# Two-layer transformer trunk on one Trainium2 core: both o-projection stages in written order with three early token tiles, the next x turned on chip, and squares, totals and o weights at other places

## The chip, the cores and the metric

One core of one Trainium2 chip runs the whole program in one launch. Its engines are TensorE (PE, matrix products), VectorE (DVE), ScalarE (ACT) and GpSimd (POOL); SyncE (SP) issues most of the DMAs. The metric is the device time of one execution in microseconds. Each engine works through its own instruction stream in order, and engines wait for one another through semaphores.

## The reference

S = 1024 tokens, D = 1024, 8 heads, a feed-forward width of 4096, all in float32. Two layers: layer A mixes tokens with multi-head latent attention, layer B with differential attention (two causal softmax maps per head). Cut to what matters:

```python
ALPHA = (2 * DEPTH) ** 0.25          # sqrt(2)
for i in range(2):
    m = (_mla if i == 0 else _diff_attn)(x, ...)      # ends with  o @ w_o
    x = layernorm(ALPHA * x + m, ln_mix_g[i], ln_mix_b[i])
    x = layernorm(ALPHA * x + square(relu(x @ w_up[i])) @ w_down[i], ln_ffn_g[i], ln_ffn_b[i])
```

A LayerNorm takes mean and variance over D of each token, with an epsilon of 1e-5 under the root.

## The kernel before

**Stages.** In the profiled execution layer A's attention runs to about 382 us, its o-projection and the start of its FFN to 516, the FFN's up loop to 806 and the down stage to 1128; then come layer B's eight heads (to 1523), the drain of the last head (to 1578), B's o-projection (to 1707), the up loop (to 1998), the down stage and the last LayerNorms (to 2310).

**Tiles.** Tokens are cut into 8 tiles of 128. Every float32 product is three fp16 products of high and low halves (`mm3`, `p3`), so each weight and each activation is scaled and split on the way: ACT writes the high half (`scaled_split`, L264) and DVE the low half (L265). `tp_...` names are transpositions on PE (eight or four 128x128 blocks); each result is evicted by ACT (L264) and DVE (L265) in the same manner.

**o-projection.** `out_proj` returns `scan` (squares of the o weights, for their scale), `scale`, `weights` (load and split of one of 8 row blocks) and `tile_steps`. For one token tile those are: `start` (load the attention's output and the residual row, and multiply the row by ALPHA on POOL, L320), eight `products` (48 matmuls of 128x512), and `end` (residual sum on DVE, L230; squares for the variance on ACT, L239; the root's few steps). `ln_apply` (L247, L250) finishes the LayerNorm on DVE. The first two tiles are done inside the attention's end, the other six after it. Each finished row X is stored to DRAM, and turned for the FFN: tiles 0 to 3 as they are (B11, B21), tiles 4 to 7 as well (B22) and as four sums with tiles 0 to 3 (T1 to T4, made by `x_sums` on POOL).

**FFN.** Up and down products use seven products in place of eight 2x2-blocked ones: for each of 16 groups g the up products are `u_p1` to `u_p7` into PSUM banks a, b, c and d; `pu` (L1039) is the ACT eviction of `u_p1`, and `u_p6` needs its bank. `u_p7(0)` is the first product of the loop over g. In that loop `up_load`, `up_sq`, `up_add`, `up_cast`, `up_scale` and `up_split` prepare the up weights three groups ahead (names `wuA_r`, `junkA`, `wuA`), `u_out` forms on POOL and stores the hidden rows (`hs`), and `wd_scan` loads the group's down weights and squares them on ACT (`wdsA`, `wdsB`). The totals of these squares give the down weights' scale (`down_scale`: reduce and cast on DVE, one matmul with ones, `tot_cd..`, then a root). The down stage takes 7 products of 8 steps (m, st_); `h16` and `w16` are the operands' splits, `add_y` (L1229) adds a product to X, and `fin_...` end the layer. In layer A `to_xt` turns each finished x for the next layer; tiles 6 and 7 are loaded again from `x1_d` at the start of the differential attention and turned there.

**Who sets the order.** A scheduler with a timeline model of its own orders each engine's instructions, except inside `with in_order():`, where PE, DVE, ACT and POOL keep the order in which the code is written. Before, the up loop, the down stage and the start of the differential attention were under it, and the o-projection stages were not. DMA queues are always the scheduler's. Of buffers, the token rows, the squares' rows (`wds`, `junk`) and the hidden rows share one ring of 8 (`row`), and raw loads of weights one of 3.

## Time and profile before

| what | value |
|---|---|
| median of 3 runs | 2306.92 us (2303.02 to 2308.64) |
| profiled execution, time | 2311.53 us |
| its span in the profile | 2309.8 us |
| mean clock granted to PE | 0.969 of full speed |
| busy: PE, DVE, ACT, POOL | 92%, 73%, 56%, 23% |

The span is the time from the first to the last instruction of the profiled execution, so 1.7 us of its time lie around it. A busy share is a mean over all stages. The granted clock of 1 stands for 2.4 GHz, and half of it for 1.2 GHz.

### The profile page before, as it was taken

To read this page: it belongs to the slowest core of one execution; us is meant where nothing else is said; L and a number is where in the kernel's file an instruction comes from. 1 tells how busy PE (TensorE), PEld (TensorE's weight loads), DVE (VectorE), ACT (ScalarE), POOL (GpSimd) and SP (SyncE) were. 2 spreads that over 40 slices of the span, in tenths; PEclk is the share of its full clock that TensorE was granted. 3 is DMA by queue.
4 is the path that set the end of the run, shared out by engine and by line. 5 is a ranking of instruction groups with operands and counts; after the bars stand their busy time and mean duration, and the time that the engine had idled before them with its cause. 6 is when DMAs were issued, how large, how long until landed. Compare 5 with 4: busy or idle time off the path is not lost. (4 is left out here: it accounts for less than half of the span.)

```text
span 2309.8 us, 31741 instructions
## 1 busy us (share of the span) xinstructions
PE 2136.2 (92%) x11255; PEld 1191.6 (52%) x11255; DVE 1684.8 (73%) x2951; ACT 1300.7 (56%) x2400; POOL 529.1 (23%) x381
## 2 busy tenths in 40 slices
PE   7999898989999899999699999969989999999997
PEld 7878775444444344444356655644444444444443
DVE  5677675767777579877578888784857776588787
ACT  5465664446666355446388777673455665354443
POOL 1101001816666310000000001000826666300000
PEclk9999999989999999999899999988989999999999
DMA  4154767526666776652565565455436666856641
GB/s 146 33 104 91 147 123 188 194 101 205 207 213 207 264 281 218 201 192 82 160 155 126 126 122 106 84 118 150 162 142 205 209 210 223 326 198 210 218 155 55
DMA packets 454831, 384.29 MB, mean 166 GB/s; under 512 B 251376, under 2 KB 346624, under 8 KB 454672
## 3 DMA queue, kind: packets, MB, share of 16 engines
q1 hardware_dynamic: 452736, 376.51, 55.2%
q0 software_dynamic: 1936, 5.75, 0.9%
q8 instruction: 88, 1.44, 0.3%
q14 instruction: 71, 0.58, 0.1%
HBM read 247.97 MB, written 83.89 MB: 144 GB/s over the span
## 5 line engine op out<-in xcount | busy, mean ns | idle before, releaser
L185 PE MATMUL yA<-w16A,h16A 128*128 128x512 f16 x1344 | 294.9, 382 | 4.4 <-DVE X2A L1229 3.1
L185 PE MATMUL yB<-w16B,h16B 128*128 128x512 f16 x1344 | 292.8, 380 | 4.6 <-DVE X2B L1229 3.1
L185 PE MATMUL qkv<-wqkv,xt_nA 128*128 128x384 f16 x1536 | 268.5, 328 | 1.0 <-DVE wqkv L265 0.7
L185 PEld LDWEIGHTS <-wuB 128*128 128x128 f16 x1344 | 132.1, 99 | 172.0 <-issue 18.1
L185 PEld LDWEIGHTS <-wuA 128*128 128x128 f16 x1344 | 132.2, 99 | 170.9 <-issue 16.0
L185 PEld LDWEIGHTS <-h16A 128*128 128x128 f16 x1344 | 132.2, 98 | 167.3 <-issue 12.5
L185 PEld LDWEIGHTS <-h16B 128*128 128x128 f16 x1344 | 131.8, 98 | 168.1 <-issue 11.4
L185 PEld LDWEIGHTS <-xt_nA 128*128 128x128 f16 x1536 | 150.0, 99 | 95.8 <-issue 4.4
L1585 DVE TENSOR_REDUCE nmx_d<-ds 128x2 f32<-128x256 f32 (+5 forms) x96 | 90.1, 951 | 24.0 <-PE ds L413 23.6
L265 DVE SCALAR_TENSOR_TENSOR h16B<-hrB,SCB,h16B 128x1024 f16<-128x1024 f32 x56 | 73.3, 1308 | 37.8 <-ACT h16B L264 37.2
L265 DVE SCALAR_TENSOR_TENSOR h16A<-hrA,SCA,h16A 128x1024 f16<-128x1024 f32 x56 | 73.8, 1317 | 35.5 <-ACT h16A L264 35.4
L264 ACT ACTIVATE h16A<-hrA,SCA 128x1024 f16<-128x1024 f32 x56 | 63.9, 1141 | 61.0 <-issue 47.9
L264 ACT ACTIVATE h16B<-hrB,SCB 128x1024 f16<-128x1024 f32 x56 | 63.9, 1140 | 59.9 <-issue 47.9
L413 PE MATMUL s<-kn,qn 128*128 128x512 f32 (+2 forms) x288 | 83.5, 385 | 8.3 <-DVE ph L427 7.8
L185 PE MATMUL oA<-woA,otA 128*128 128x512 f16 x384 | 86.7, 387 | 4.1 <-DVE ph L427 4.1
L185 PE MATMUL oB<-woB,otB 128*128 128x512 f16 x384 | 85.4, 379 | 0.0
L265 DVE SCALAR_TENSOR_TENSOR wuB<-wuB_s,cuB,wuB 128x1024 f16<-128x1024 f32 (+1 forms) x32 | 56.7, 1771 | 34.9 <-ACT wuB L264 34.9
L185 PE MATMUL av_d<-pt16d,dv 128*128 128x256 f16 (+1 forms) x480 | 59.3, 277 | 24.4 <-DMA pt16d<-phd 24.4
L265 DVE SCALAR_TENSOR_TENSOR wuA<-wuA_s,cuA,wuA 128x1024 f16<-128x1024 f32 (+1 forms) x32 | 54.9, 1716 | 34.9 <-ACT wuA L264 34.9
L264 ACT ACTIVATE w16B<-wdB,RBB 128x1024 f16<-128x1024 f32 x40 | 45.7, 1142 | 53.5 <-DVE wdB L1186 53.5
L264 ACT ACTIVATE w16A<-wdA,RBA 128x1024 f16<-128x1024 f32 x40 | 45.7, 1141 | 53.4 <-DVE wdA L1186 53.4
L1489 POOL MEMSET ones_f<- 128x128 f32 x1 | 0.2, 205 | 305.3 <-PE yA L185 305.3
(876 smaller groups left out, 5099.1 us busy)
## 6 DMA issues: line engine op xcount, KB each, us to landing
hrA<-hs_d SPq DMA_DIRECT2D x56, 512.0 KB, 3.8
hrB<-hs_d SPq DMA_DIRECT2D x56, 512.0 KB, 3.8
wuA_r<-in_ffn_w_up_dram SPq DMA_DIRECT2D x32, 512.0 KB, 4.5
wdsA<-in_ffn_w_down_dram SPq DMA_DIRECT2D x32, 512.0 KB, 6.5
wdA<-in_ffn_w_down_dram SPq DMA_DIRECT2D x32, 512.0 KB, 4.7
wuB_r<-in_ffn_w_up_dram SPq DMA_DIRECT2D x32, 512.0 KB, 4.3
wdsB<-in_ffn_w_down_dram SPq DMA_DIRECT2D x32, 512.0 KB, 5.9
wdB<-in_ffn_w_down_dram SPq DMA_DIRECT2D x32, 512.0 KB, 4.6
```

The source lines that it names most:

```text
L185: nc.tensor.matmul(dst, l, r, start=first and m == 0, stop=last and m == n - 1, skip_group_check=resumed)
L264: nc.scalar.mul(hi, src, scale)
L265: nc.vector.scalar_tensor_tensor(out=lo, in0=src, scalar=scale, in1=hi, op0=ALU.mult, op1=ALU.subtract)
L413: nc.tensor.matmul(dst, q_, k_(c0 // 512, n), start=m == 0, stop=m == len(pairs) - 1)
L1489: nc.gpsimd.memset(ones_f, 1.0)
L1585: nc.vector.tensor_reduce(out=nmx[:, ms], in_=st["wide"][:, :, :nk] if i < 4 else st[m], axis=AX.X, op=ALU.max, negate=True)
```

## The change

The residual is no longer multiplied by ALPHA: the o-projection's and the down stage's scales are divided by ALPHA instead, and the LayerNorm's epsilon by ALPHA squared, which gives the same LayerNorm. After the attention both o-projection stages stand under `in_order()`, and a third token tile moves inside the attention's end. The load of the squares' rows (`wd_fetch`) is cut from the squares (`wd_scan`); the reduce and cast of the down scale (`down_sum`) stand earlier than its matmul. Tiles 6 and 7 of the next x are turned right after their LayerNorm. Layer B's o weights are scanned and loaded one head earlier.

The diff, cut to its core:

```diff
+            nc.vector.tensor_scalar(out=icw, in0=icw, scalar1=1.0 / ALPHA, scalar2=None, op0=ALU.mult)
...
-                nc.gpsimd.tensor_scalar(out=t["x"], in0=t["x"], scalar1=ALPHA, scalar2=None, op0=ALU.mult)
...
-            def end():
-                nmean = residual(t["y"], icw, t["x"], f"m{nm}{i}")
-                st[i] = t["x"], nmean, ln_stats(t["x"], nmean, t["y"], f"m{nm}{i}")
-
-            return [(0.1, start)] + [(1.3, lambda k=k: products(k)) for k in range(H)] + [(0.1, end)]
+            def sums():
+                t["m"] = residual(t["y"], icw, t["x"], f"m{nm}{i}")
+
+            def squares():
+                t["q"] = ln_ssq(t["x"], t["m"], t["y"], f"m{nm}{i}")
+
+            def root():
+                st[i] = t["x"], t["m"], rstd_of(t["q"], 1.0 / D, LN_EPS_A, f"ln_m{nm}{i}")
...
+                + [(0.1, sums), (0.1, squares), (0.1, root)]
...
+            return o_steps(u - 3, lambda: x_t(u - 3)) if u - 3 < 3 else []
...
+            def wd_fetch(g):
+                wds[g] = [row(f"wds{nm}{g}{f_}") for f_ in range(2)]
+                for f_ in range(2):
+                    nc.sync.dma_start(out=wds[g][f_], in_=wdn[:, g, f_, :])
+
             def wd_scan(g):
...
-                for f_ in range(2):
-                    wr = row(f"wds{nm}{g}{f_}")
-                    nc.sync.dma_start(out=wr, in_=wdn[:, g, f_, :])
+                for f_, wr in enumerate(wds.pop(g)):
                     nc.scalar.activation(wr, wr, AF.Square, accum_out=wdsq[g // 2][:, 2 * (g % 2) + f_ : 2 * (g % 2) + f_ + 1])
...
-            new_xc()
-            order = [0, 1, 4, 5, 2, 6, 3, 7]
-            for n, i in enumerate(order):
-                X[i] = row(f"X{nm}{i}")
-                if n >= n_early:
-                    for _, step in o_steps(i, lambda i=i: X[i]):
-                        step()
+            order = [0, 1, 2, 4, 5, 6, 3, 7]
...
+            def begin(n):
+
+                if n < NT:
+                    i = order[n]
+                    X[i] = row(f"X{nm}{i}")
+                    if n >= n_early:
+                        todo[n] = [step for _, step in o_steps(i, lambda: X[i])]
+                        todo[n].pop(0)()
...
-                if n == 2:
-                    up_load(0)
-                    up_sq(0)
-                    up_add(0)
-                    up_cast(0)
...
-                    up_add(2)
...
+            def turn(n):
...
-                    to_xc("B11", X[i], i)
-                    to_xc("B21", X[i][:, 512:], i)
-                else:
-                    if n == NT - 1:
-                        for g in range(2):
-                            u_p1(g)
-                            u_p2(g)
-                    t = x_sums(i - 4, nc.gpsimd if n < NT - 1 else nc.vector)
-                    for key, src in (("T2", t[:, 1]), ("T1", t[:, 0]), ("T3", t[:, 2]), ("T4", t[:, 3]), ("B22", X[i][:, 512:])):
-                        to_xc(key, src, i - 4)
-
-
-            wd_scan(0)
-            u_p6(0)
-            u_p5(0)
...
+                    return [lambda: to_xc("B11", X[i], i), lambda: to_xc("B21", X[i][:, 512:], i)]
+                t = xsum[i - 4]
+                rows = (("B22", X[i][:, 512:]), ("T2", t[:, 1]), ("T1", t[:, 0]), ("T3", t[:, 2]), ("T4", t[:, 3]))
+                return [lambda key=key, src=src: to_xc(key, src, i - 4) for key, src in rows]
...
+            prepare = {
+                3: ([lambda: up_prepare(0)], []),
+                4: ([lambda: up_cast(0)], [lambda: up_scale(0), lambda: up_split(0, 0), lambda: up_split(0, 1)]),
+                5: ([lambda: up_split(0, 2), lambda: up_split(0, 3)], [lambda: up_prepare(1)]),
+                6: ([lambda: up_cast(1)], [lambda: up_scale(1)]),
+                7: ([], [lambda: wd_fetch(0), lambda: up_load(2), lambda: (up_sq(2), up_add(2)), lambda: wd_scan(0)]),
+            }
+            with in_order():
+                for n in range(n_early + 2):
+                    begin(n)
+                for n in range(n_early):
+                    normal(n)
+                new_xc()
+                for n in range(n_early, NT + 1):
+                    begin(n + 2)
+                    before, after = prepare.get(n, ([], []))
+                    for step in before:
+                        step()
+                    turns = turn(n - 2)
+                    if n == n_early:
+                        turns = turn(0) + turns
+                    if n < NT:
+                        for _ in range(4):
+                            todo[n].pop(0)()
+                    else:
+                        for step in turns:
+                            step()
+                        turns = []
+                        u_p1(0)
+                        u_p2(0)
+                    if n > n_early:
+                        sums_, squares_, root_ = todo[n - 1]
+                        sums_()
+                        squares_()
+                    if turns:
+                        turns.pop(0)()
+                    else:
+                        up_split(1, 0)
+                    if n > n_early:
+                        root_()
+                        normal(n - 1)
+                        if order[n - 1] >= 4:
+                            i = order[n - 1] - 4
+                            xsum[i] = x_sums(i, nc.gpsimd if n < NT else nc.vector)
+                    if n < NT:
+                        for step in todo[n][:4]:
+                            step()
+                        del todo[n][:4]
+                    for step in turns + after:
+                        step()
+                u_p1(1)
+                u_p2(1)
+                for step in turn(NT - 1):
+                    step()
+                u_p6(0)
+                up_split(1, 1)
+                u_p5(0)
+                up_split(1, 2)
+                up_split(1, 3)
+
...
                     if g + 3 < NG:
                         up_load(g + 3)
                     if g + 1 < NG:
-                        wd_scan(g + 1)
+                        wd_fetch(g + 1)
                     if w:
                         up_cast(g + 2)
+                    if g == NG - 2:
+                        down_sum(NA, "A")
                     if 0 < g < NG - 1:
                         u_p1(g + 1)
...
                         u_p5(g + 1)
+                        wd_scan(g + 1)
                     u_out(g)
...
-                    if (m, st_) == (0, 4):
-                        for i in range(NT):
-                            nc.scalar.mul(X[i], X[i], ALPHA)
...
+                    if (m, st_) == (0, 0):
+                        down_sum(NS, "B")
                     if (m, st_) == (0, 2):
                         down_scale(NS, "B")
...
-                            if layer == 0 and i > 0:
+                        else:
+                            if layer == 0 and i in (1, 2):
                                 to_xt(xt_n, i - 1, "n", ps_wide)
-                        else:
                             fin_rstd(i)
                             fin_apply(i)
-                    if m == 6 and st_ == 1 and layer == 0:
-                        to_xt(xt_n, 3, "n")
+                    if m == 6 and st_ in (1, 2) and layer == 0:
+                        to_xt(xt_n, 1 + st_, "n")
...
+                if layer == 0:
+                    to_xt(xt_n, 6, "n")
                 fin_apply(7)
+                if layer == 0:
+                    to_xt(xt_n, 7, "n")
...
+            if (h, u) in ((H - 2, 0), (H - 2, 2)):
+                steps = merge(steps, [(0.1, lambda k=k: wo_scan(k)) for k in range(2 * u, 2 * u + 4)])
+            if (h, u) == (H - 2, 3):
+                steps.append((0.1, wo_scale))
             if h == H - 1:
-                steps += [(0.1, lambda k=k: wo_scan(k)) for k in range(4 * u, 4 * u + 4)]
+                steps = merge(steps, [(0.1, lambda k=k: wo_load(k)) for k in range(2 * u, 2 * u + 2)])
...
-                return [(0.1, wo_scale)] + [(0.1, lambda k=k: wo_load(k)) for k in range(H)]
+                return [(0.1, lambda k=k: wo_load(k)) for k in range(4, H)]
...
+            return [s for i in range(*((0, 1), (1, 3))[u - 3]) for s in o_steps(i, lambda: x_t(i))]
...
-            xn = [wp.tile([P, D], F32, tag="raw", name=f"x1_{t}", bufs=3) for t in range(2)]
-            for t in range(2):
-                nc.gpsimd.dma_start(out=xn[t], in_=x1_d[(6 + t) * P : (7 + t) * P, :])
...
-                if t in (1, 2):
-                    transpose_in16(xn[t - 1], xt1[1], t + 1, f"nA{5 + t}", sx[:, 2:3])
...
-    mixer_out_and_ffn(1, ws, None, o_steps, o_state, 2, out[0], "B")
+    mixer_out_and_ffn(1, ws, None, o_steps, o_state, 3, out[0], "B")
```

**The up loop.** The squares keep their place on ACT; their loads move against the weights' loads. ACT in the first iteration of the loop of layer A, before (`junk` are squares of the up weights read by `wuA_r`, `pu` the eviction for which `u_p6` waits):

```order
L940 ACTIVATE junkA_5558,wssqA_5557<-wuA_r_5482 128x1024
L940 ACTIVATE junkA_5558,wssqA_5557<-wuA_r_5483 128x1024
L1080 ACTIVATE hA_5376<-hA_5376 128x512
L1081 ACTIVATE hA_5376,hsA_5552<-hA_5376 128x1024
L264 ACTIVATE wuA_3_5582<-wuA_s_5259,cuA_5509 128x512
L1122 ACTIVATE wdsA_5615,wdsqA_5614<-wdsA_5615 128x1024
L1122 ACTIVATE wdsA_5618,wdsqA_5614<-wdsA_5618 128x1024
L1039 ACTIVATE puA_5635<-abA_5349,cuA_5509 128x512
```

ACT at the same place now:

```order
L949 ACTIVATE junkA_5550,wssqA_5549<-wuA_r_5476 128x1024
L949 ACTIVATE junkA_5550,wssqA_5549<-wuA_r_5477 128x1024
L1089 ACTIVATE hA_5348<-hA_5348 128x512
L1090 ACTIVATE hA_5348,hsA_5544<-hA_5348 128x1024
L265 ACTIVATE wuA_3_5574<-wuA_s_5299,cuA_5501 128x512
L1136 ACTIVATE wdsA_5480,wdsqA_5304<-wdsA_5480 128x1024
L1136 ACTIVATE wdsA_5481,wdsqA_5304<-wdsA_5481 128x1024
L1048 ACTIVATE puA_5626<-abA_5321,cuA_5501 128x512
```

SP's queue before, around the load that those squares read (`wdsA_5615` and `wdsA_5618`):

```order
L1121 DMA wdsA_5486<-in_ffn_w_down_dram 128x1024
L1121 DMA wdsA_5489<-in_ffn_w_down_dram 128x1024
L1121 DMA wdsA_5615<-in_ffn_w_down_dram 128x1024
L1121 DMA wdsA_5618<-in_ffn_w_down_dram 128x1024
L931 DMA wuA_r_5610<-in_ffn_w_up_dram 128x8x128
L931 DMA wuA_r_5611<-in_ffn_w_up_dram 128x8x128
```

SP's queue now, around the load that they read now (`wdsA_5480` and `wdsA_5481`):

```order
L940 DMA wuA_r_5476<-in_ffn_w_up_dram 128x8x128
L1307 DMA x_d<-XA_4937 128x1024
L1129 DMA wdsA_5480<-in_ffn_w_down_dram 128x1024
L1129 DMA wdsA_5481<-in_ffn_w_down_dram 128x1024
L1183 DMA wrA_7640<-in_ffn_w_down_dram 128x4x512
L940 DMA wuA_r_5477<-in_ffn_w_up_dram 128x8x128
L1129 DMA wdsA_5608<-in_ffn_w_down_dram 128x1024
```

Before, the squares' load was the last one asked for ahead of them, and stood ahead of `wuA_r_5610`, the weights of group 3. Now it stands one iteration earlier; the load that now has the old place (`wdsA_5608`, `wdsA_5609`) is squared an iteration later.

**The end of o-projection A.** ACT before, from the evictions of the last tile but one to those of the last (`tp_fA3B` and `tp_fA3T` are the transpositions of tiles 3 and 7, `puA` and `hA` evictions of `u_p1` and `u_p2`):

```order
L264 ACTIVATE xB22A<-tp_fA2B_5176,xs_c 128x4x128
L264 ACTIVATE xB11A<-tp_fA3B_5264,xs_c 128x4x128
L264 ACTIVATE xB21A<-tp_fA3B_5271,xs_c 128x4x128
L1039 ACTIVATE puA_5362<-abA_5349,cuA_4883 128x512
L264 ACTIVATE xT2A<-tp_fA3T_5414,xs_c 128x4x128
L264 ACTIVATE xT1A<-tp_fA3T_5421,xs_c 128x4x128
L1048 ACTIVATE hA_5376<-abA_5349,cuA_4883 128x512
L1039 ACTIVATE puA_5392<-abA_5379,cuA_5117 128x512
L264 ACTIVATE xT3A<-tp_fA3T_5428,xs_c 128x4x128
L264 ACTIVATE xT4A<-tp_fA3T_5435,xs_c 128x4x128
L1048 ACTIVATE hA_5406<-abA_5379,cuA_5117 128x512
```

ACT now, from the same point:

```order
L265 ACTIVATE xT4A<-tp_fA2T_5279,xs_c 128x4x128
L949 ACTIVATE junkA_5295,wssqA_5294<-wuA_r_5290 128x1024
L949 ACTIVATE junkA_5295,wssqA_5294<-wuA_r_5291 128x1024
L1136 ACTIVATE wdsA_5286,wdsqA_5304<-wdsA_5286 128x1024
L1136 ACTIVATE wdsA_5287,wdsqA_5304<-wdsA_5287 128x1024
L265 ACTIVATE xB11A<-tp_fA3B_5307,xs_c 128x4x128
L265 ACTIVATE xB21A<-tp_fA3B_5314,xs_c 128x4x128
L1048 ACTIVATE puA_5334<-abA_5321,cuA_4921 128x512
L1057 ACTIVATE hA_5348<-abA_5321,cuA_4921 128x512
L240 ACTIVATE oA_5185,lnsq_mA_5354<-XA_4937,rsum_mA_5351 128x1024
L265 ACTIVATE wuA_0_5356<-wuA_r_5053,cuA_5175 128x1024
L161 ACTIVATE t_ln_mA_5361<-y_ln_mA_5359 128x1
```

Two squares of up weights and two of down weights now stand ahead of the evictions of tile 3 (`xB11A`, `xB21A`), and the last tile's square and a first split of the second group's up weights (`wuA_0_5356`) between the first `hA` and the second `puA`.

**The boundary between the layers.** ACT before, at the start of layer B (`qk_0`, `dv` evict the first products there, `xt_nA` the transposed x):

```order
L1514 ACTIVATE qk_0_10218<-qkv_0_10192 128x256
L1516 ACTIVATE dv_10217<-qkv_0_10192 128x128
L1514 ACTIVATE qk_0_10218<-qkv_1_10222 128x256
L1516 ACTIVATE dv_10217<-qkv_1_10222 128x128
L1540 CAST dz_0_10251<-qk_0_10218 128x2x4x64
L264 ACTIVATE xt_nA_10056<-tp_nA_10260,xs_c 128x4x128
L264 ACTIVATE xt_nA_10057<-tp_nA_10267,xs_c 128x4x128
L295 ACTIVATE woB0s_raw,fwB<-woB0s_raw,gsub 128x1024
L295 ACTIVATE woB1s_raw,fwB<-woB1s_raw,gsub 128x1024
```

ACT now, after the last apply:

```order
L161 ACTIVATE t_ln_fA_10133<-y_ln_fA_10131 128x1
L162 ACTIVATE r_ln_fA_10132<-t_ln_fA_10133 128x1
L265 ACTIVATE xt_nA_10044<-tp_nA_10140,xs_c 128x4x128
L265 ACTIVATE xt_nA_10045<-tp_nA_10147,xs_c 128x4x128
L265 ACTIVATE xt_nA_10044<-tp_nA_10157,xs_c 128x4x128
L265 ACTIVATE xt_nA_10045<-tp_nA_10164,xs_c 128x4x128
L1590 ACTIVATE qk_0_10230<-qkv_0_10204 128x256
L1592 ACTIVATE dv_10229<-qkv_0_10204 128x128
L1590 ACTIVATE qk_0_10230<-qkv_1_10234 128x256
```

and the o weight scans, now in the down stage of layer A:

```order
L296 ACTIVATE woB0s_raw,fwB<-woB0s_raw,gsub 128x1024
L161 ACTIVATE t_ln_fA_9539<-y_ln_fA_9537 128x1
L162 ACTIVATE r_ln_fA_9538<-t_ln_fA_9539 128x1
L265 ACTIVATE h16A_9576<-hrA_9486,SCA 128x1024
L296 ACTIVATE woB1s_raw,fwB<-woB1s_raw,gsub 128x1024
L296 ACTIVATE woB2s_raw,fwB<-woB2s_raw,gsub 128x1024
L265 ACTIVATE w16A_9577<-wdA_9488,RBA 128x1024
L296 ACTIVATE woB3s_raw,fwB<-woB3s_raw,gsub 128x1024
L1270 ACTIVATE ljA_9585,fsq_A_9584<-X2A_7913,rsum_fA_9582 128x1024
L265 ACTIVATE h16A_9613<-hrA_9549,SCA 128x1024
```

The transpositions of tiles 6 and 7 now come ahead of the first products' evictions and wait for no load; the eight scans left this place (`woB0s` to `woB7s`) and now stand between splits of the last products' operands.

## Rows read from the trace of the kernel before

**Rows 1.** page, part 1: busy time, share of the span, instructions of each engine

```profile
PE 2136.2 (92%) x11255; PEld 1191.6 (52%) x11255; DVE 1684.8 (73%) x2951; ACT 1300.7 (56%) x2400; POOL 529.1 (23%) x381
```

**Rows 2.** windows (start:end, length, busy us and count per engine, PE clock, DMA share, GB/s)

```profile
418.00:516.00 98.00, 86.40 (x427) 45.69 (x426) 71.66 (x107) 42.29 (x77) 51.13 (x29) 0.91 0.36 128
516.00:806.00 290.00, 279.10 (x1288) 126.12 (x1286) 199.43 (x293) 172.11 (x279) 176.16 (x110) 0.99 0.64 217
1128.00:1155.00 27.00, 13.12 (x74) 8.40 (x73) 13.79 (x27) 11.34 (x24) 1.11 (x2) 0.68 0.70 210
1523.00:1579.00 56.00, 31.14 (x146) 17.67 (x144) 42.09 (x85) 37.77 (x81) 0.00 (x0) 0.66 0.57 131
1613.00:1707.00 94.00, 85.11 (x426) 45.15 (x425) 70.43 (x108) 44.06 (x82) 52.69 (x32) 0.93 0.45 153
```

**Rows 3.** waits of PE in the up loops: total us, times, longest

```profile
PE abA L185 <- ACT puA L1039: 8.7, 6, 4.4
PE tot_cdAA L274 <- DVE totb_cdAA L269: 1.2, 1, 1.2
...
PE abB L185 <- ACT puB L1039: 8.3, 5, 4.5
```

**Rows 4.** waits of ACT, up loop of layer A

```profile
ACT wdsA L1122 <- issue: 8.8, 10, 2.5
ACT wdsA L1122 <- DMA wdsA<-in_ffn_w_down_dram: 7.3, 4, 4.7
```

**Rows 5.** timeline of PE in the up loops (start, us, ..., idle before it)

```profile
763.22 5.28 PE L185 MATMUL abA<-xT2A,wuA 128*128 128x512 f16 x12 [4.35 <-ACT puA L1039]
...
1764.90 4.33 PE L185 MATMUL abB<-xT2B,wuB 128*128 128x512 f16 x12 [1.91 <-ACT puB L1039]
...
1956.34 4.44 PE L185 MATMUL abB<-xT2B,wuB 128*128 128x512 f16 x12 [4.49 <-ACT puB L1039]
```

**Rows 6.** timeline of PE at the down scale's totals

```profile
826.32 0.16 PE L274 MATMUL tot_cdAB<-totb_cdAB,ones_b 128*128 128x1 bf16 x1 [2.82 <-DVE totb_cdAB L269]
826.34 7.03 PE L185 MATMUL yA<-w16A,h16A 128*128 128x512 f16 x24
...
2018.17 0.16 PE L274 MATMUL tot_cdBB<-totb_cdBB,ones_b 128*128 128x1 bf16 x1 [2.82 <-DVE totb_cdBB L269]
```

**Rows 7.** waits of PE at the end of the first down stage

```profile
PE tp_nA L216 <- DVE X2A L250: 5.7, 3, 3.0
```

**Rows 8.** timeline of DVE, then PE, at the boundary between the layers

```profile
1136.62 1.28 DVE L250 SCALAR_TENSOR_TENSOR X2A<-X2A,r_ln_fA,lnfbA 128x1024 f32<-128x1024 f32 x1
...
1142.28 1.94 PE L216 MATMUL tp_nA<-ident_r,x 128*128 128x128 f32 x8 [13.88 <-DMA x<-x_d]
1144.01 6.08 PE L185 MATMUL qkv<-wqkv,xt_nA 128*128 128x384 f16 x24
```

**Rows 9.** the tile woB in the last head (durations in ns; then who waits)

```profile
L264 ACT ACTIVATE woB<-woB3w_raw,fwB x1: 1147/1147/1147, 1539.9 to 1539.9; 128x1024 f16<-128x1024 f32 x1
L265 DVE SCALAR_TENSOR_TENSOR woB<-woB3w_raw,fwB,woB x1: 1283/1283/1283, 1541.1 to 1541.1; 128x1024 f16<-128x1024 f32 x1
  DMA woB3w_raw<-in_diff_w_o_dram: 4.4, 1
  PE ds L413: 4.5, 1
```

**Rows 10.** timeline of PE at the end of o-projection A

```profile
507.90 2.75 PE L185 MATMUL abA<-xT2A,wuA 128*128 128x512 f16 x12
...
516.11 1.24 PE L185 MATMUL abA<-xT3A,wuA 128*128 128x512 f16 x5
```

**Rows 11.** timeline of DVE and ACT, o-projection A

```profile
468.50 1.28 DVE L265 SCALAR_TENSOR_TENSOR wuA<-wuA_r,cuA,wuA 128x1024 f16<-128x1024 f32 x1 [0.93 <-ACT wuA L264]
...
496.14 0.69 ACT L264 ACTIVATE xB11A<-tp_fA3B,xs_c 128x512 f16<-128x512 f32 x1 [1.75 <-PE tp_fA3B L1001]
```

**Rows 12.** groups by line, ACT, o-projection A (busy us, mean ns)

```profile
L940 ACT ACTIVATE junkA<-wuA_r 128x1024 bf16<-128x1024 f32 x4 | 4.2, 1057 | 10.2 <-DMA wuA_r<-in_ffn_w_up_dram 6.0 <-issue 4.2
```

More of the change, by code (lines that the diff above doesn't have):

```diff
@@ L141, in consts @@
         return t
+    LN_EPS_A = LN_EPS / ALPHA ** 2
     eps_t = consts("eps_t", [LN_EPS, RMS_EPS])
@@ L332, in products @@
                     )
-            def end():
-                nmean = residual(t["y"], icw, t["x"], f"m{nm}{i}")
-                st[i] = t["x"], nmean, ln_stats(t["x"], nmean, t["y"], f"m{nm}{i}")
-            return [(0.1, start)] + [(1.3, lambda k=k: products(k)) for k in range(H)] + [(0.1, end)]
+            def sums():
[4 more added lines that the diff above has]
+                st[i] = t["x"], t["m"], rstd_of(t["q"], 1.0 / D, LN_EPS_A, f"ln_m{nm}{i}")
+            return (
+                [(0.1, start)]
+                + [(1.3, lambda k=k: products(k)) for k in range(H)]
+                + [(0.1, sums), (0.1, squares), (0.1, root)]
+            )
         return scan, scale, weights, tile_steps, st
@@ L879, in x_t @@
             def x_t(i):
-                if i == 0:
-                    early["x"] = xtp.tile([P, 2, D], F32, tag="xt", name="x_early")
-                return early["x"][:, i]
-            return o_steps(u - 3, lambda: x_t(u - 3)) if u - 3 < 2 else []
+                if i % 2 == 0:
+                    early["x"] = xtp.tile([P, 2, D], F32, tag="xt", name=f"x_early{i}")
+                return early["x"][:, i % 2]
+            return o_steps(u - 3, lambda: x_t(u - 3)) if u - 3 < 3 else []
         first = mla_filler(-1, 2) + mla_filler(-1, 3) + mla_filler(0, 0)
@@ L1118, in wd_scan, with down_sum, down_scale @@
                     wdsq[g // 2] = fp.tile([P, 4], F32, tag="wdsq", name=f"wdsq{nm}{g}", bufs=3)
[L1119 to L1121 removed]
+                for f_, wr in enumerate(wds.pop(g)):
                     nc.scalar.activation(wr, wr, AF.Square, accum_out=wdsq[g // 2][:, 2 * (g % 2) + f_ : 2 * (g % 2) + f_ + 1])
[L1124 removed]
+            tb = {}
+            def down_sum(n, key):
                 tsum = fp.tile([P, 1], F32, tag="tsum", name=f"tsum{nm}{key}", bufs=2)
                 nc.vector.tensor_reduce(out=tsum, in_=c1["T"][:, :n], axis=AX.X, op=ALU.add)
[L1128 to L1132 removed]
+                tb[key] = total_in(tsum, f"cd{nm}{key}")
+            def down_scale(n, key):
+                pn = total_out(tb[key], f"cd{nm}{key}", ps_mm if key == "A" else ps_wide)
+                inv_root(c1["cd" + key], pn, 1.05 * D_SPREAD / F16_TOP ** 2)
+                icd = c1["icd" + key]
+                nc.vector.reciprocal(icd[:, 1:2], c1["cd" + key])
+                for n_, sign in ((0, 1.0 / ALPHA), (1, -1.0 / ALPHA)):
+                    nc.vector.tensor_scalar(
+                        out=icd[:, n_ : n_ + 1], in0=icd[:, 1:2], scalar1=sign, scalar2=None, op0=ALU.mult
+                    )
                 nc.vector.tensor_scalar(
@@ L1252, in fin_rstd @@
                 nmean, ssq = fin[i]
[L1253 removed]
+                fin[i] = nmean, rstd_of(ssq, 1.0 / D, LN_EPS_A, f"ln_f{nm}{i}")
             def fin_apply(i):
```

45 lines of the change are left out of this document (16 added, 29 removed).

## The prediction, written before the changed kernel ran

> **What bounds the kernel now.** The page comes first: TensorE (PE) is busy 92% of the span, VectorE (DVE) 73%, ScalarE (ACT) 56% and GpSimd (POOL) 23% [rows 1]. No edit here removes a matmul, so only three things can move the time: PE's idle stretches, the clock it is granted behind them, and waits that are new. The share of 92% is a mean, so I cut the span by stage [rows 2]. In the FFN's up loop PE is nearly full (279.10 of 290 us at clock 0.99). It is not in the two o-projection stages (11.6 us idle of 98 in layer A, 8.9 of 94 in layer B, clocks 0.91 and 0.93), at the boundary between the layers (13.9 idle of 27, 0.68), and in the last head's drain (24.9 idle of 56, 0.66). Then the list of waits says who PE waits for in each stage, the timeline what stood on the releasing engine, and the order of rows (shown with the change) what stands there now.
>
> **The change, part by part.**
>
> *Squares of the down weights.* In the up loops PE waits 8.7 us in layer A and 8.3 in layer B for `pu`, an ACT eviction [rows 3]. ACT is late because it stands in front of the two `wds` squares just ahead of `pu`: it waits 7.3 us for their DMA, 4.7 in one piece, and 8.8 for their "issue" [rows 4]. The new order leaves the squares at the very same place, but their load starts one iteration (290 us for 16 groups, 18 us) earlier. I take these waits as gone but for 1 us in each layer: −15. Behind the long waits twelve matmuls took 5.28, 4.33 and 4.44 us [rows 5] where twelve at full clock take 2.75 [rows 10]: 2.5 + 1.6 + 1.7 = 5.8, so −6. Together **−21**. Bounds: −11 if only ACT's waits for DMA go and the rest is the tightness of the place (two squares at 1.06 us [rows 12] still stand ahead of `pu`), −24 if all goes with the slow matmuls after them.
>
> *Totals for the down scale.* PE waits 1.2 us for `tot_cdAA` [rows 3], I count as much in layer B, and 2.82 for `tot_cdAB` and again for `tot_cdBB` [rows 6]: 8.0. All four wait for a reduce and a cast on DVE, which now stand one or two steps earlier. Behind one of the long waits 24 matmuls took 7.03 us against 2 × 2.75: 1.5, twice. That makes 11.0; I take **−10**. Bounds: −4 (only part of each wait; the clock stays) and −11.
>
> *The boundary.* `to_xt` of tiles 0 to 2 stands one step later, when the apply it waits for has ended: PE's 5.7 us of waits for DVE there [rows 7] go. Tiles 6 and 7 are no longer stored and loaded again: PE stood 13.88 us for that load, until 1142.28, while DVE's last apply ended at 1136.62 + 1.28 = 1137.9 [rows 8]. The next products started at 1144.01; with eight transpositions (1.94 at half clock) and an eviction (0.7, as in [rows 11]) behind the apply they start at about 1137.9 + 1.9 + 0.7 = 1140.5, and the second eight, which now stand between products, come before: −4 to −5. Eight scans of the o weights (ACT, some 1.1 each) leave the start of the attention, where ACT waited for their DMAs: −2. They arrive in the down stage between `h16A` and `w16A`, and their loads stand on SP's queue ahead of the last two `hrA` loads; 8 × 1.1 on an engine that is 56% busy [rows 1] should hide, but it can be late by a DMA for some `h16A`, and products wait for that: +3. Sum **−10**. Bounds: −16 (nothing lost) and −2 (two of these scans hold a product for 4 us each, as a late o weight held PE for 4.5 [rows 9]).
>
> *The last head's drain.* Eight o weight loads (ACT 1.15, DVE 1.28 each [rows 9], so some 9 and 10 us) leave the last head for the head before. In the drain PE waited 4.5 us for one of them, and ACT 4.4 for its DMA [rows 9]. The chain of softmax, DMA and weighted values remains, and holds PE's other waits. I take 4.5 and part of a slow matmul stretch: **−7**. Bounds: −15 (all the ACT time was on the chain) and +3 (head 6, which has PE at work throughout, has no room for them).
>
> *Written order in the o-projections.* The same products, transpositions and evictions remain, so PE's busy time stays; what changes is its idle time, 11.6 us now in A. I walked the new rows from the point where 144 of 384 products are done (three tiles, in both kernels at about 418), with the prices of [rows 11, 12]. Waits that I find: 1.7 at the first normalisations, which stand behind a residual on DVE; 5.6 in the iteration in which DVE gets four splits of up weights (3 × 1.28 and a half) beside residual, two applies and ten evictions, about as much as PE's 48 matmuls and 20 transpositions, so that evictions are late and the two transposition banks stay full; 1 in each of the next two; then, after the last product, 6.8: ACT has four squares of 1.06 us and their read-outs (5.0 in all) ahead of the two evictions for which `u_p1(0)` waits; and 4.9 ahead of `u_p1(1)`, whose weights' first split now stands behind the last tile's square on ACT and its copy on DVE. Sum 21.0, against 11.6: +9. The first `u_p7`, at 516.1 now [rows 10], would come at about 525. B has the same rows: 21.0 against 8.9, +12. Together **+21**. Bounds from the same rows: −20 if no wait is left at all, +35 if the walk misses 3.5 us at each of two tiles per stage (a split of weights with its ACT half late).
>
> The walk speaks of new idle stretches, and rows 5 show matmuls behind a 4.35 us wait at half speed. The Trainium skill has that as a rule ("TensorE: Matmul & The Clock Gate", section "HAM oscillation — how this bites in real kernels"): a loop that lets PE stand while it waits pays a cold start each time. By the rule the stage after is slower than its waits alone; I keep it out of the sum, because the stage of before has such stretches too (clock 0.91), and give it a chance of its own below.
>
> *At nothing.* POOL's multiplications of the residual by ALPHA go (POOL is busy 51.13 of 98 us there [rows 2] and hardly waited for); the factor goes into three tiny DVE operations. Without that cover they would be worth a few us in each stage. The ACT multiplications by ALPHA in the down stage go where PE doesn't wait for ACT.
>
> Sum: −21 − 10 − 10 − 7 + 21 = **−27**. The profiled execution took 2311.5 us; that is 4.6 above the median of 2306.9, from which I count: 2306.9 − 27 = **2280**.
>
> **The rivals.**
> *(a) The written order costs nothing.* DVE and ACT may take the splits and squares in the shade of PE, so that the stages keep the idle time that they have. For it: DVE's work in the stage (71.66 of 98 us [rows 2]) leaves room. Against: the walk, in which the room lies at other places than the load. Then −48 and 2259.
> *(b) The squares' wait stays.* For it: the place on ACT is the same, and part of the wait is called "issue", not DMA. Then −27 + 21 = −6: 2301, no change that a measurement of this kernel (about 0.3%, 7 us) can tell.
> *(c) Each new gap is followed by slow matmuls.* Three gaps of about 5 us in each stage, each with a stretch at half clock that costs 2.5 [rows 5, 10]: 3 × 2 × 2.5 = 15 more, so −12 and 2295. For it: row 763.22. Against: the stage of before already holds such stretches. It is the page's rule told in this kernel's rows.
> *(d) Slower: DVE bounds the written order.* In the written order no engine may take a later row first. If each of the five tiles that are normalised inside the stage stalls PE like the one with the splits, 5.6 us rather than the 1 to 2 found for the others, that is some 4 × 4.2 × 2 = 34 more: +7, 2314. The other edits cancel at 27 us more over both stages, 2.7 for each tile.
>
> **How the numbers follow.** The forecast, as summed, 0.43; (a) 0.20; (b) 0.13; (c) 0.13; (d) 0.11. Faster by over 0.3% (below 2300): nearly all of the forecast, (a) and most of (c), a third of (b): 0.78. Same: the rest of (b) and (c): 0.12. Slower: most of (d): 0.10. The range from 2254 to 2305 takes in (a) with a few us of the drain's bound, and (b); it leaves out (d) and little else.
>
> **What would show it.** In the up loops the waits for `puA` and `puB` fall from 17 us to about 2 and the twelve-matmul rows behind them take 2.75; the four `tot_cd` waits are below 1; PE's stand of 13.9 at the boundary is near 10; no o weight stands in the last head. The last `oA` ends near 486 instead of 477 when counted from the same start, ACT shows two `wds` squares before the evictions of tile 3, and PE's idle time in each o-projection stage is about 21 us. It would be wrong if those stages' idle time falls (then the time is near 2259), if `pu` is still waited for, or if `h16A` waits for the scans in the down stage of layer A.

## The result, and the profile after

The changed kernel took 2314.5 us (median of 6 runs, 2313.57 to 2318.09) against 2305.6 for the kernel before in the same runs: ratio 1.0042, 95% interval 1.0029 to 1.0056, so 9 to 10 us slower. The forecast was 2280, and its range ended at 2305.

The traces add up to it. The table cuts the span at the first or last start of a matmul on a tile, as the tile view lists them. It has three profiles of before (spans 2309.8, 2304.2, 2300.6) and two of after (2314.3, 2309.2), in us:

| from, to | before | after |
|---|---|---|
| o-projection A: first `oA`, first `u_p7` | 134.1, 133.8, 134.1 | 148.5, 148.0 |
| up loop A: to the first `yA` | 290.3, 286.8, 287.9 | 279.1, 278.5 |
| down A: to the last `yA` | 320.7, 320.8, 320.8 | 320.4, 321.2 |
| boundary: to the first `av_d` | 51.6, 52.0, 51.0 | 44.6, 44.5 |
| layer B's heads, drain, o-projection: to the first `u_p7` | 528.4, 528.1, 528.4 | 553.9, 549.1 |
| up loop B: to the first `yB` | 291.1, 288.0, 284.1 | 279.7, 279.8 |
| down B: to the last `yB` | 299.9, 299.8, 300.3 | 295.1, 295.1 |

In the means the two o-projection rows lose 14 and 23, and the others gain 29; another 1.2 are gained ahead of the first `oA`. That is 7 us in the spans, and 9 in the medians. The waits that the forecast wanted gone from the up loops are gone. PE's waits there, layer A and then layer B (total us, times, longest), are the whole list and answer to [rows 3]; no `puA`, no `puB` and no `tot_cd` is left:

```profile
PE tot_wuA L275 <- DVE totb_wuA L270: 1.6, 4, 0.9
PE yA L186 <- DVE hA L1039: 1.3, 1, 1.3
PE abA L186 <- ACT hA L1057: 1.1, 2, 0.6
...
PE tot_wuB L275 <- DVE totb_wuB L270: 1.7, 5, 0.9
PE yB L186 <- DVE hB L1039: 1.3, 1, 1.3
PE abB L186 <- ACT hB L1057: 1.1, 2, 0.6
```

The loss is in the windows of the two written stages of after (length, then busy us of PE, PEld, DVE, ACT, POOL, the clock), which answer to the first and last of [rows 2]:

```profile
418.00:530.00 112.00, 90.32 (x424) 44.92 (x423) 66.75 (x111) 47.66 (x84) 32.31 (x24) 0.89 0.40 132
...
1609.00:1728.00 119.00, 94.40 (x430) 47.06 (x429) 66.16 (x113) 48.58 (x87) 29.87 (x24) 0.87 0.39 123
```

PE is idle 21.7 us in A (11.6 before) and 24.6 in B (8.9 before): +10 and +16. It is also busy 3.9 and 9.3 us longer with about the same matmuls, at a lower clock. The second profile of after, cut at the same rows, has nearly the same idle time (21.7 and 25.0) and is busy 3.7 and 5.3 us longer; its B stage has the clock of before, 0.93:

```profile
417.50:529.30 111.80, 90.11 (x425) 44.80 (x423) 66.80 (x111) 47.65 (x84) 32.36 (x24) 0.89 0.41 133
1607.20:1722.60 115.40, 90.39 (x428) 45.75 (x427) 65.95 (x113) 48.44 (x87) 29.86 (x24) 0.93 0.40 127
```

Idle and slow stretches are seen in the timeline of PE, layer A, first profile:

```profile
460.81 1.94 PE L1010 MATMUL tp_fA0T<-ident_r,xsumA 128*128 128x128 f32 x8 [3.78 <-DVE xT2A L266]
462.54 6.21 PE L186 MATMUL oA<-woA,otA 128*128 128x512 f16 x24
...
497.59 0.58 PE L186 MATMUL abA<-xB11A,wuA 128*128 128x512 f16 x1 [3.42 <-ACT xB11A L265]
498.37 4.22 PE L186 MATMUL abA<-xB11A,wuA 128*128 128x512 f16 x11 [0.20 <-DVE xB11A L266]
503.37 2.75 PE L186 MATMUL abA<-xB21A,wuA 128*128 128x512 f16 x12 [0.78 <-ACT puA L1048]
509.13 1.04 PE L186 MATMUL abA<-xB11A,wuA 128*128 128x512 f16 x2 [3.00 <-ACT wuA L265]
510.45 4.45 PE L186 MATMUL abA<-xB11A,wuA 128*128 128x512 f16 x10 [0.28 <-DVE y_ln_mA L160]
```

In this stage each stand of 3 to 4 us (a stretch in which PE is idle) is followed by matmuls at half speed: ten take 4.45 where twelve take 2.75 a little earlier. What PE stood for at 497.59 is on ACT, in the order that the change shows:

```profile
492.57 1.05 ACT L949 ACTIVATE junkA<-wuA_r 128x1024 bf16<-128x1024 f32 x1
...
494.79 1.04 ACT L1136 ACTIVATE wdsA<-wdsA 128x1024 f32<-128x1024 f32 x1
...
495.83 1.04 ACT L1136 ACTIVATE wdsA<-wdsA 128x1024 f32<-128x1024 f32 x1
...
496.87 0.67 ACT L265 ACTIVATE xB11A<-tp_fA3B,xs_c 128x512 f16<-128x512 f32 x1
```

Layer B has one wait more, which no row of layer A shows at that size: the first up weights' squares stand ahead of the first evictions and wait for their load, and the load is later there. ACT, then PE:

```profile
1621.43 1.06 ACT L949 ACTIVATE junkB<-wuB_r 128x1024 bf16<-128x1024 f32 x1 [5.99 <-DMA wuB_r<-in_ffn_w_up_dram]
...
1624.33 0.67 ACT L265 ACTIVATE xB11B<-tp_fB0B,xs_c 128x512 f16<-128x512 f32 x1
...
1625.84 1.97 PE L1010 MATMUL tp_fB1B<-ident_r,XB 128*128 128x128 f32 x8 [5.10 <-DVE xB11B L266]
```

The second profile of after has this wait too, at 5.3 us; the 24 matmuls of 128x512 behind it take 7.34 us in the first profile and 6.26 in the second, so one and the same stand has not one price. At the boundary PE's long stand for the reload [rows 8] became two shorter ones, and waits stand ahead of them, in the down stage:

```profile
1070.10 5.12 PE L186 MATMUL yA<-w16A,h16A 128*128 128x512 f16 x23 [2.72 <-DVE w16A L266]
...
1086.82 1.97 PE L217 MATMUL tp_nA<-ident_r,X2A 128*128 128x128 f32 x8 [4.61 <-DVE xt_nA L266]
...
1124.44 5.34 PE L186 MATMUL yA<-w16A,h16A 128*128 128x512 f16 x24 [3.12 <-DVE X2A L1251]
...
1136.63 1.94 PE L217 MATMUL tp_nA<-ident_r,X2A 128*128 128x128 f32 x8 [5.98 <-DVE y_ln_fA L160]
1142.74 1.94 PE L217 MATMUL tp_nA<-ident_r,X2A 128*128 128x128 f32 x8 [4.17 <-DVE X2A L251]
1146.44 9.87 PE L186 MATMUL qkv<-wqkv,xt_nA 128*128 128x384 f16 x48 [1.76 <-DVE dv L1593]
```

Not every stand has slow matmuls behind it: here 24 take 5.34 us, full speed, behind 3.12 us, and 23 take 5.12 behind 2.72.

### The profile page after: what moved, and what is told of

The parts are those of the page before. It is cut to its first block, busy times and chain, and to the rows that moved or that the text cites. A ratio compares the mean times of both kernels' runs of the same rounds, so it can differ in the third digit from the quotient of the medians.

```text
span 2314.3 us, 31747 instructions
## 1 busy us (share of the span) xinstructions
PE 2136.1 (92%) x11255; PEld 1186.8 (51%) x11255; DVE 1676.9 (72%) x2957; ACT 1284.1 (55%) x2384; POOL 483.9 (21%) x363
## 5 line engine op out<-in xcount | busy, mean ns | idle before, releaser
L423 PE MATMUL ds<-qkT 128*128 128x128 f16 (+3 forms) x256 | 59.8, 315 | 14.6 <-DVE p_d L1679 14.2
```

Source lines behind the costliest of these rows:

```text
L423: nc.tensor.matmul(dst, q_, k_(c0 // 512, n), start=m == 0, stop=m == len(pairs) - 1)
```

## The experiments

Times are ratios to the kernel before, run on the same chip, with 95% intervals; 0.001 is 2.3 us. The medians of before were 2303.0 in the first four runs, 2305.7 in the next four, 2305.5 in the four after.

**The old o-projection stages** (`old_oproj`): all other edits of the change stay.

```diff
-            order = [0, 1, 2, 4, 5, 6, 3, 7]
-            with in_order(): ...            # the stage as written
+            order = [0, 1, 4, 5, 2, 6, 3, 7]
+            for n, i in enumerate(order): ...   # the stage of before
-    mixer_out_and_ffn(1, ws, None, o_steps, o_state, 3, out[0], "B")
+    mixer_out_and_ffn(1, ws, None, o_steps, o_state, 2, out[0], "B")
```

> The changed kernel with both o-projection stages as they were (scheduler's order, two early token tiles, old tile order); all other edits stay. Theory: the written order's new waits and the slow matmuls behind them cost about 38 us in the two stages, and the rest of the change gains about 34, so this comes to 2314.5 - 38 = 2276 us, 1.3% below the kernel before; the up loops start at about 516 and 1700 and last 279 us each as in the changed kernel. Rival: the up loops are shorter only because the written stage did part of their work ahead; then they last 290 us again and the time is that of before, about 2305.

Measured: 0.9862 (0.9843 to 0.9881), 2270.7 us. That is 0.018, or 41 us, below the changed kernel. Its up loops last 278.5 us each, so the rival falls: the loops' gain doesn't hang on the written stage. Its o-projection A lasts 129.9 us, 4 less than before, and with the old stage it lasts 128 to 130 in every run below that has the change's other edits, against 133.7 in `fetch_only`. What the change leaves inside that stage is mainly the removal of ALPHA, which the prediction put at nothing: POOL is relieved, and PE's wait of 1.8 us for POOL's sums there is gone. No run tests ALPHA alone.

**The new code, ordered by the scheduler** (`free_oproj`).

```diff
-            with in_order():
+            with nullcontext():
                 for n in range(n_early + 2):
```

> The changed kernel with its new o-projection code (three early tiles, cut steps), but the stage no longer held to the written order: the scheduler orders it. Theory (the order is what costs): within 10 us of the kernel with the old stages, 2276 to 2286. Rival (the third early tile and the new tile order cost, whoever orders them): about 2314, as the changed kernel.

Measured: 0.9922 (0.9898 to 0.9946), 2284.7 us. So most of the 41 us is the order as written (28), and some 14 come with the new code, whoever orders it; which part of that code costs them (the third early tile, the new order of tiles, the cut steps), no run tells.

**The written order repaired** (`written_fix`).

```diff
-                3: ([lambda: up_prepare(0)], []),
-                4: ([lambda: up_cast(0)], [lambda: up_scale(0), lambda: up_split(0, 0), lambda: up_split(0, 1)]),
-                5: ([lambda: up_split(0, 2), lambda: up_split(0, 3)], [lambda: up_prepare(1)]),
-                6: ([lambda: up_cast(1)], [lambda: up_scale(1)]),
-                7: ([], [lambda: wd_fetch(0), lambda: up_load(2), lambda: (up_sq(2), up_add(2)), lambda: wd_scan(0)]),
+                3: ([lambda: up_load(0)], [lambda: (up_sq(0), up_add(0))]),
+                4: ([lambda: up_cast(0)], [lambda: up_scale(0), lambda: up_split(0, 0)]),
+                5: ([lambda: up_split(0, 1)], [lambda: up_split(0, 2), lambda: up_prepare(1)]),
+                6: ([lambda: up_split(0, 3), lambda: up_cast(1)], [lambda: up_scale(1)]),
+                7: ([], [lambda: up_split(1, 0), lambda: wd_fetch(0), lambda: up_load(2)]),
...
                 up_split(1, 3)
+                up_sq(2)
+                up_add(2)
+                wd_scan(0)
```

> The changed kernel, written order kept, with the steps moved that stand ahead of what PE waits for: the squares of the third up weights and the first down weights behind the stage's last evictions, the first split of the second up weights one tile earlier, the first up weights' squares behind the first evictions, the four splits of the first up weights spread over three tiles. Theory: the waits of 3.4 and 3.0 in each stage, the 5.1 in layer B's and half of the 3.8 in each go, 22 us in all, and some 6 us of slow matmuls with them: about 2287. Rival (the waits only move, since DVE and ACT have no room for the same work elsewhere): 2305 to 2314.

Measured: 0.9999 (0.9986 to 1.0011): 10 us gained, not 27. The waits that were aimed at went or shrank (the 5.10 in B to 1.1), and new ones came, in PE's timeline:

```profile
479.52 1.75 PE L1010 MATMUL tp_fA1T<-ident_r,xsumA 128*128 128x128 f32 x8 [2.92 <-DVE xT2A L266]
...
510.16 2.75 PE L186 MATMUL abA<-xB11A,wuA 128*128 128x512 f16 x12 [1.95 <-ACT oA L240]
```

The wait of 3.78 ahead of the first T rows' second half stayed to the hundredth, though two of the four splits had left that iteration. So those two splits were not its cause. In the changed kernel's trace DVE stands idle 1.88 us between the splits and the next evictions, and then runs both steps of a tile's apply (2 x 1.28) ahead of the eviction for which PE waits:

```profile
455.56 0.75 DVE L266 SCALAR_TENSOR_TENSOR xB22A<-tp_fA0B,xs_c,xB22A 128x512 f16<-128x512 f32 x1 [1.88 <-ACT xB22A L265]
...
457.40 1.28 DVE L248 SCALAR_TENSOR_TENSOR XA<-XA,rsum_mA,lnmgA 128x1024 f32<-128x1024 f32 x1
458.71 1.28 DVE L251 SCALAR_TENSOR_TENSOR XA<-XA,r_ln_mA,lnmbA 128x1024 f32<-128x1024 f32 x1
459.91 0.75 DVE L266 SCALAR_TENSOR_TENSOR xT2A<-tp_fA0T,xs_c,xT2A 128x512 f16<-128x512 f32 x1
```

The up loops became 2 to 3 us longer (282.0 and 281.5), where PE now waits up to 2.8 us for the total of the up weights' squares (`tot_wu`, at most 0.9 in the changed kernel).

**Matmuls in the stands** (`warm`): they compute nothing that is kept.

```diff
+                if g < 2:
+                    lh = wts[0][0]["S1"][0]
+                    for _ in range((16, 14)[g]):
+                        nc.tensor.matmul(bank[g]["a"], lh[:, 0, :], lh.rearrange("p k n -> p (k n)"), start=True, stop=True)
                 prod(bank[g]["a"], "A11", "B11", g)
```

> The changed kernel with matmuls added whose results are overwritten: 16 of 128x512 ahead of the first up product of group 0 and 14 ahead of that of group 1 in each layer, where PE stood 3.4 and 3.0 us. Theory (the stand itself brings the slow clock, at some 2 us for each of the four places): 8 us less than the changed kernel, 2306, with both twelve-matmul stretches at 2.75 instead of 4.8 and 5.5. Rival (the stretches are long because their operands come late): 2314 or a little more.

Measured: 1.0019 (1.0007 to 1.0030), 5 us below the changed kernel. From the last `oA` to the first `u_p7` it takes 37.5 us in both layers, where the changed kernel takes 41.7 and 41.9 (41.6 and 40.1 in its second profile): 7 to 9 together. PE's timeline (L1049 are the added matmuls):

```profile
496.27 3.62 PE L1049 MATMUL abA<-wuA 128*128 128x512 f16 x16
...
500.64 2.53 PE L186 MATMUL abA<-xB11A,wuA 128*128 128x512 f16 x11 [0.41 <-DVE xB11A L266]
...
511.68 2.75 PE L186 MATMUL abA<-xB11A,wuA 128*128 128x512 f16 x12
```

The eleven matmuls that took 4.22 take 2.53, the last twelve 2.75. The granted clock over 418 to 530 us is 0.98 in place of 0.89. So PE's idleness brings the slow stretch here, and not operands that come late.

**The scans of the o weights** (`pin`, on `old_oproj`).

```diff
-            if (h, u) in ((H - 2, 0), (H - 2, 2)):
-                steps = merge(steps, [(0.1, lambda k=k: wo_scan(k)) for k in range(2 * u, 2 * u + 4)])
...
             for t in range(4):
                 for _, step in qkv_steps(0, t):
                     step()
+                if t > 1:
+                    for k in range(4):
+                        wo_scan(4 * t - 8 + k)
```

> The kernel with the old o-projection stages (old_oproj), and the eight scans of layer B's o weights held to the start of the differential attention, behind the first products' evictions, where they stood before. Theory: in the changed kernel they slipped into layer A's down stage because the reload of x no longer held two of the three raw buffers, and there they make the operands' splits late (waits of 0.7, 2.7 and 4.6 us and some 2 us of slow matmuls): about 9 us less than old_oproj, 2262. Rival: the scans cost as much at the start of the attention: no change, 2271.

Measured: 0.9875 (0.9852 to 0.9897), no better than `old_oproj`. The down stage does get 7.0 us shorter (313.2 against 320.2), but the boundary 10.7 longer (55.3 against 44.6). The mechanism was right, the price was not: the scans cost as much at the start of the attention, where PE then waits 3.3 us for a DMA of the first scores' operands.

**The last apply ahead of the transposition** (`pin_apply` on `pin`, and `o_apply` on `old_oproj`).

```diff
-                    to_xt(xt_n, 6, "n")
                 fin_apply(7)
                 if layer == 0:
+                    to_xt(xt_n, 6, "n")
                     to_xt(xt_n, 7, "n")
```

> pin, and the last LayerNorm's apply of tile 7 written ahead of tile 6's transposition (it stood behind tile 6's eviction on VectorE). Theory: the apply comes 2.5 us earlier and so does tile 7's transposition: 2 to 3 us less than pin, 2260. Rival: tile 6's transposition then comes as much later, and both evictions still stand ahead of the first products' evictions: no change.

> The kernel with the old o-projection stages and the apply of tile 7 ahead of tile 6's transposition; the scans stay in the down stage. Theory: as between pin_apply and pin, 2 us at the boundary: 2269. Rival: nothing, 2271.

Measured: 0.9834 (0.9813 to 0.9856) and 0.9843 (0.9830 to 0.9857). The boundary is 2.1 us shorter than in `pin`, and 0.9 shorter than in `old_oproj`. The rest of the step from `pin` is elsewhere: its heads (first `av_d` to first `oB`) last 7 us less and the stretch behind them 3 more, in an order that the scheduler chose anew. Against `old_oproj` the two intervals overlap.

**The reload of x** (`o_reload`) and **the o weights in the last head** (`o_wolate`), each undone on `old_oproj`; then both (`o_rl_wl`).

```diff
+            xn = [wp.tile([P, D], F32, tag="raw", name=f"x1_{t}", bufs=3) for t in range(2)]
+            for t in range(2):
+                nc.gpsimd.dma_start(out=xn[t], in_=x1_d[(6 + t) * P : (7 + t) * P, :])
...
+                if t in (1, 2):
+                    transpose_in16(xn[t - 1], xt1[1], t + 1, f"nA{5 + t}", sx[:, 2:3])
...
-                return [(0.1, lambda k=k: wo_load(k)) for k in range(4, H)]
+                return [(0.1, wo_scale)] + [(0.1, lambda k=k: wo_load(k)) for k in range(H)]
```

> The kernel with the old o-projection stages, with x of tiles 6 and 7 stored, loaded again and turned in the attention's start as before; the two reloaded rows take two of the three raw buffers, so the scans stay there too. Against pin it tells what the turn on chip is worth by itself. Theory (by the ledger of the traces the turn only moves PE's stand, since tile 7's apply now waits for tile 6's eviction and the first products' evictions stand behind both): 0 to 2 us more than pin. Rival (the prediction): 5 us more than pin.

> The kernel with the old o-projection stages, with layer B's o weights scaled and loaded inside the last head as before. Theory (prediction's term, and 5 us in the ledger): 5 us more than old_oproj, 2276. Rival: the ACT and DVE time is as dear in the head before: no change.

> The kernel with the old o-projection stages, the old place of all o weight work and the reload of x as before, so that of the change only the split loads, the earlier totals, the removal of ALPHA and the later turns of tiles 0 to 3 are left. Theory (turn on chip and o weights are worth nothing measurable): as old_oproj, 2271, 1.4 to 1.6% below before. Rival (the prediction's 7 for the drain and 5 for the boundary): 2280.

Measured: 0.9837 (0.9816 to 0.9858), 0.9858 (0.9836 to 0.9880) and 0.9836 (0.9821 to 0.9851). None of the three is slower than `old_oproj`; with the reload the medians are even some 6 us lower, at the edge of what the intervals can tell, and `o_reload` is 9 us faster than `pin`, where it was expected to be 0 to 5 slower. So neither the turn on chip nor the earlier o weights is worth anything that these runs can measure.

**The split loads alone** (`fetch_only`, on the kernel before), and undone (`o_fetch`, on `old_oproj`).

```diff
-                        wd_scan(g + 1)
+                        wd_fetch(g + 1)
...
                         u_p5(g + 1)
+                        wd_scan(g + 1)
```

> The kernel before with one edit alone: the load of the squares' rows cut from the squares and asked for one iteration earlier. Theory (the load was late, not ACT): the waits for pu of 17 us in both up loops go but for some 3, and the slow matmuls behind them; the two up loops take 280 us each instead of 290: 2285, 0.9% below before. Rival (the place on ACT is what is tight, and the gain in the changed kernel has other causes): within 5 us of before.

> The kernel with the old o-projection stages, with the squares put back to the top of the iteration, right behind their load's start. Theory: the up loops are 290 us again, so 2271 + 22 = 2293. Rival: they stay at 279, because the totals and the other edits made them shorter; 2271.

Measured: 0.9945 (0.9931 to 0.9958) and 0.9903 (0.9886 to 0.9920). The edit alone brings 13 us: its up loops last 280.5 each. PE's waits in its first loop, all of them:

```profile
PE tot_wuA L274 <- DVE totb_wuA L269: 1.6, 4, 1.0
PE tot_cdAA L274 <- DVE totb_cdAA L269: 1.2, 1, 1.2
PE abA L185 <- ACT hA L1048: 1.1, 2, 0.6
```

Undoing it costs 9, and the loops last 283.6 and 285.8, not 290; the waits for `pu` are back, 5.4 and 4.0 us.

**Two more profiles of before, one of after.**

> The kernel before, unchanged, profiled a second time. Its first profile took 2311.5 us, 6 above its median. If that execution was long for its waits on the squares' loads, this one shows less than 17 us of waits for pu in the two up loops and up loops below 290; if the waits are the kernel's own, they read 17 again and the 5 us lie elsewhere.

> The kernel before, unchanged, profiled a third time, with the same two readings: under 17 us of waits for pu where the first execution was long for them, 17 again where they are the kernel's own.

> The changed kernel, unchanged, profiled a second time: the two written stages last as in its first profile (first oA to first u_p7 148 us in layer A), since their waits come from the order of the rows and not from loads, except the 5.1 us wait behind the up weights' load in layer B.

PE's waits for `puA` and `puB`, second profile of before, then the third:

```profile
PE abA L185 <- ACT puA L1039: 5.2, 6, 1.8
...
PE abB L185 <- ACT puB L1039: 6.3, 5, 4.1
```

```profile
PE abA L185 <- ACT puA L1039: 7.5, 7, 3.2
...
PE abB L185 <- ACT puB L1039: 4.4, 6, 1.5
```

11.5 and 11.9 us, where the first profile had 17.0. The waits are the kernel's own, their length differs between executions, and the prediction read the longest of three. The written stages of after repeat within 0.5 us in A. In B the second profile is 3.5 us shorter from the wait of 5 us to the first `u_p7`, with nearly the same idle time and less busy time.

## Why the prediction was wrong

**The sum's last term failed: "PE's busy time stays; what changes is its idle time", +21.** By the windows it measured +39 in the first profile and +35 in the second; the two o-projection rows of the table, which hold the drain too, lost 37. In layer A the walk's sum was right: idle time is 21.7, forecast 21.0, with 5.5 (1.68 + 3.78) where 5.6 was expected, 5.8 in four pieces for 6.8 and 4.1 in three for 4.9. What failed first was the half of the sentence on busy time: PE is busy 3.9 us longer in A and 9.3 (second profile: 5.3) in B, by slow matmuls behind gaps. That was rival (c), given 15 us and a chance of 0.13 and left out of the sum because the stage of before has slow stretches too. `warm` shows the cause at four of the places. The Trainium skill has it as a rule (page "TensorE: Matmul & The Clock Gate", section "HAM oscillation — how this bites in real kernels"): a loop in which the matmuls wait starts at the slow clock again after each such wait. The trace agrees in layer A, with a clock of 0.89 against 0.91; in B it is 0.87 in one profile and 0.93, that of before, in the other, and the stand of 3.12 us in the down stage had no slow matmuls behind it. The second failure is B: "B has the same rows". It has, but the rows wait for a load that comes later there, 5.1 us.

The step that named the four splits as the cause of the 5.6 us in one iteration is also wrong: with two of them elsewhere the wait of 3.78 was the same. That 5.5 was found there is luck. It is also by chance that the time is the one of rival (d), 2314: by (d) DVE stalls PE for 5.6 us at every normalised tile, and in layer A PE's waits for DVE at the tiles after that one are 0.2 to 2.5 us each.

**The boundary: −10 forecast, about −3 measured.** Down A and the boundary together fall from 372.3 to 365.4, of which the total `tot_cdAB` is worth some 4 (2.82 us of wait and its slow matmuls, as forecast). The scans cost 7.0 us in the down stage (`pin`), not 3, and operands that come late for them there were a sign of being wrong that the prediction named; at the attention's start they cost the boundary 10.7, not 2. Of the 5.7 us of waits for tiles 0 to 2, 3.0 are left without the scans (`pin`). The turn's −5 came to nothing: with the scans at the attention's start the boundary lasts 55.3 us with the turn (`pin`) and 52.8 with the reload (`o_reload`). PE's stand of 13.88 became 5.98, 4.17 and 1.76, since tile 7's apply waits for tile 6's eviction, and the first products' evictions now stand behind both.

**The drain: −7 forecast, none found.** The o weights left the last head, and PE now waits there for DVE's probabilities, 14.4 us where it had waited 7.7. PE's waits in the drain, all of them, before and after:

```profile
PE av_d L185 <- DMA pt16d<-phd: 9.3, 4, 3.2
PE ds L413 <- DVE p_d L1603: 7.7, 3, 3.6
PE ds L413 <- ACT woB L264: 4.5, 1, 4.5
PE av_d L1620 <- ACT sq L1614: 3.4, 2, 2.2
```

```profile
PE ds L423 <- DVE p_d L1679: 14.4, 3, 8.3
PE ds L423 <- ACT p_d L1666: 7.9, 3, 3.2
PE av_d L186 <- DVE rec_d L1682: 1.9, 1, 1.9
PE av_d L1696 <- ACT sq L1690: 0.6, 1, 0.6
```

They add up to 24.9 us before and 24.8 after. `o_wolate` is not slower than `old_oproj`. So the 4.5 us stand for a late weight hid other waits of the same length; that they are the softmax chain's is read from the lists, and no run took it away.

**The up loops (−21) and the totals (−10) were right in their place and for the first profile:** −22.6 in the loops, with the first totals' waits (forecast 2.4), and −4.8 in down B. Against the mean of three profiles the loops gave −17.5: the price was read from the execution with the longest waits. The rival that the squares' place is what is tight falls with `fetch_only`, since no wait for `pu` is left at the same place. But in the loops of the profiles `fetch_only` takes 15 us off that mean and `o_fetch` gives only 12 back. The difference of some 3 us is no more than the same loop differs between the three profiles of before (3.5 us in A, 7.0 in B).

All in all the edits other than the o-projection's gained about 32 us (`old_oproj`), where the forecast had 48 for them, and the new o-projection stages took 41, where it had 21. The 32 hold some 4 us in o-projection A that the forecast did not have, having put the removal of ALPHA at nothing.

## What to carry to other kernels

A new idle stretch of TensorE is priced with the slow matmuls that can stand behind it (here 0 to 3 us each); one that is removed, too. Where an order is written by hand, look for work that nobody waits for soon (squares, splits of the next weights) standing on an engine ahead of an eviction that PE waits for, and ask of each row that reads a load whether that load is as early in every layer. Before a wait that hangs on a DMA is counted as a gain, take more than one profile: here it was 11.5 to 17.0 us in three.

The version to keep is the old o-projection stage with the rest of the change. With the reload and the o weights as before, it takes 2265.5 us, 1.6% below the kernel before, and the plainer code costs nothing.

## What was not expected of the hardware

Matmuls that compute nothing made a stage shorter: with 30 more of them in each layer the stretch from the last o-projection product to the loop fell by 4.1 to 4.2 us in A and by 2.6 to 4.4 in B, against the two profiles of the changed kernel. The slow matmuls behind one and the same stand differ between executions of one kernel: behind 5.1 and 5.3 us, 24 took 7.34 and 6.26 us. And a buffer set the place of unrelated work: without the reloaded rows two of three raw buffers were free, and the scheduler moved eight scans a stage ahead (in `old_oproj` they start from 1025 to 1048 us, with the reload, in `o_reload`, from 1124 to 1144).
